# Which stages carry a decoder trunk's modulation rows, in which buffers, and the order at two stage ends

## The chip, the cores and the metric

The kernel runs on one core of one Trainium2 chip. The core has a matrix engine (PE, with a weight-load port of its own, PEld), a vector engine (DVE), a scalar engine (ACT), a general engine (POOL) and a sync engine (SP); each works through its own queue in order. Loads are issued from the SP and POOL queues and carried by 16 DMA engines. Tiles lie in on-chip memory, 128 partitions by so many elements; products accumulate in a second memory, PSUM (tiles named ps_...). The metric is the device time of one execution in microseconds (us); the median of several runs counts.

## The reference

Two layers, each a feed-forward block (half weight), a mixing block and another feed-forward block, on a sequence of 512 tokens with 1024 channels. Each block normalises its input and shifts and scales it; its output goes through a gate. These nine vectors of 1024 a layer, the modulation, come from one vector c:

```python
c_act = jax.nn.silu(c)
for l in range(DEPTH):                                   # 2
    mod = (c_act @ w_ada[l] + b_ada[l]).reshape(B, N_MOD, D_MODEL)      # 9 x 1024
    sh1, sc1, gt1, sh2, sc2, gt2, sh3, sc3, gt3 = [mod[:, i, None, :] for i in range(N_MOD)]
    hn = rms_norm(h, g_ffn1[l]) * (1.0 + sc1) + sh1
    h = h + 0.5 * (1.0 + gt1) * swiglu(hn, w_ffn1_in[l], w_ffn1_out[l])
    hn = rms_norm(h, g_mix[l]) * (1.0 + sc2) + sh2
    proj = hn @ w_mix_in[l]
    ...                            # attention, RWKV recurrence, short convolution, out product
    h = h + (1.0 + gt2) * mixed
    hn = rms_norm(h, g_ffn2[l]) * (1.0 + sc3) + sh3
    h = h + 0.5 * (1.0 + gt3) * swiglu(hn, w_ffn2_in[l], w_ffn2_out[l])
```

with `swiglu(x, w_in, w_out) = (silu(x @ w_in's first half) * (x @ w_in's second half)) @ w_out`, 2816 wide inside, all float32.

## The kernel before

**Tiling.** The state is kept transposed in eight tiles h of 128 x 512 (1024 channels by 512 tokens). Float32 products run as three products of a shorter format: every operand is split into a high part (wH, hnH, xs) and the rest (wL, hnL). `split` (L105 to L107) does this for a weight tile of 128 x 1024: ACT casts it to wH, DVE subtracts to get wL, PE uses wH, then wL.

**Stages.** In order: ffn1 of layer 0 (another routine, `ffn`), then for the rest mix 0, ffn2 of layer 0, ffn1 of layer 1, mix 1, ffn2 of layer 1. These three feed-forward stages are `ffn_whole`. It makes 22 column tiles of the wide product in pairs p = 0 to 10. Pairs 0 and 1 are done plainly (four column tiles j = 0 to 3, L1053 on; their stage start). Pairs 2 to 10 (`pair_in`) and the product back to 1024 channels (`out_product`) use Strassen-like sums: fewer products, with sums of weight blocks in their place, made by accumulating loads on POOL (`accum_op`) and by DVE additions. `out_product` runs seven products (A0, S, A1, S0, S1, S3, A3), each over six units u of two of the eleven row blocks k (the last unit has one); its weight row tiles are called rowk, 128 x 512.

**The modulation.** Each of its vectors is a column of eight values per partition; one value column needs one dot product on DVE (`ada_dot`, L170, a SCALAR_TENSOR_TENSOR of 128 x 1024 with an accumulated output): a 512 KB row tile of w_ada against silu(c) spread over the partitions (crow). 128 such rows remain for the kernel's stages after the start (`todo`), 16 having been done before. `ffn` of layer 0 does 48 of them beside its own work. `ffn_whole` does the rest by a plan (`ada_plan`, L197): DOTS says how many dots belong to each pair p, ROWS which of eight buffers b their row tiles use. The buffers are slots of later pairs' results (raw in the profile), so fewer are free toward the end. `load` issues a row's load on POOL for pairs up to one ahead, when its buffer has no earlier dot outstanding; `dots` puts each dot behind given instructions. In the table, DOTS[1] = (0, 6, 4, 4, 4, 4, 4, 4, 3, 2, 1): six dots at the plain start (two behind j = 2, four behind j = 3, L1074), then 30. DOTS[0], for the last stage, holds the last eight. Two crow tiles are loaded on SP, one for the six, one for the others. The mixes do no dots.

**Order.** A scheduler sets the order in most places from the code's order and its priorities, with buffers as constraints. At the end of the first two `ffn_whole` stages (`out_product`, L1016 on) the order is written by hand: `update` adds the block's result to h, `square` and `total` sum squares for the next norm, `stats` and `spread` make the reciprocal root (ACT's rstd, PE's ps_ss and ps_rstd), `apply` writes the next stage's normalised tiles hnH and hnL, `prepare` splits weights and sums of the remaining units, and `ahead` splits the first weight tiles of the stage that follows.

**The mix.** `products` (a generator in `mix`) yields the column tiles in the order of TILES: key, value, q0 to q3, lo, k0, r0, v0 and so on, weights from SP, while the attention and the two halves of the recurrence are interleaved. Tiles with tag u1 (four buffers) serve the second half of the recurrence later.

Of the kernel before, what the change touches and what calls it, by code (L numbers as in the profile page):

```python
# [36 lines left out]
DOTS = ((0, 0, 2, 2, 2, 2), (0, 6, 4, 4, 4, 4, 4, 4, 3, 2, 1))  # L37
ROWS = {1: (0, 1, 2, 3), 2: (0, 1, 2, 3), 3: (0, 1, 2, 3), 4: (2, 3, 4, 5), 5: (2, 3, 4, 5), 6: (4, 5, 6, 7), 7: (4, 5, 6, 7), 8: (5, 6, 7), 9: (6, 7), 10: (7,)}
# [24 lines left out]
def trunk_kernel(ctx, tc, ins, out, layers=L, phases=("ffn1", "mix", "ffn2")):  # L63
# [134 lines left out]
    def ada_plan(plan, bufs, crow):  # L198

        begun, last, marked = {}, [], set()  # L200
        turns = {}
        for p, n in enumerate(plan):
            for _ in range(n):
                own = ROWS[p]
                turns[p] = turns.get(p, -1) + 1
                last.append((p, own[(turns[p] + 2 * (p == 2 and plan[1] > 0)) % len(own)], todo.pop(0)))
        left, loaded, done = list(range(len(last))), {}, [0]
        rows = {}
# [10 lines left out]
        def dot(p, behind=None):  # L219
# [7 lines left out]
            with tc.issue_after(behind.ins) if behind else nullcontext():  # L227
                ada_dot(mod[l, i][:, k : k + 1], rows[n], crow[p > 1])
# [432 lines left out]
    def ffn_whole(l, w_in, w_pair, w_s, hn, im, ss, need, then, ready):  # L661
# [4 lines left out]
        with tc.tile_pool(name="act", bufs=1) as ap_:  # L666
# [66 lines left out]
            plan_ = DOTS[len(todo) > 8]  # L733
            crow = {}
            if plan_[1]:
                crow[False] = flat(R[1][:, 1])
                nc.sync.dma_start(crow[False], silu_c[0])
            load_rows, dot_ = ada_plan(plan_, [flat(R[n // 2][:, n % 2]) for n in range(4, 4 + 8)], crow)
# [74 lines left out]
            def out_product(rest):  # L813
# [19 lines left out]
                def load(name, u):  # L833
# [6 lines left out]
                    elif name == "S3":  # L840
                        for k in ks:
                            queued(nc.gpsimd, kept[k], block(one(k), 1, 0), accum_op=ALU.add)
# [155 lines left out]
                stats, spread, apply, low_, ahead = then()  # L998
                raws = [wp.tile([P, KD, P], F32, name="wraw", tag="wraw", bufs=2) for _ in range(2)]
                raws.append(flat(spare[3]).rearrange("p (k c) -> p k c", c=P))  # L1000

                def update(q, m):
                    pt = plan[q][2]
                    half, sl, _ = plan[q][4][0]
                    i = 4 * half + m
                    stt(h[i][:, sl], pt[m // 2][:, m % 2], cg[:, i : i + 1], h[i][:, sl], ALU.mult, ALU.add)
                    return square(i, sl)

                def total(sq, sl):
                    tt(ss[:, sl], ss[:, sl], sq, ALU.add)  # L1010
# [5 lines left out]
                with tc.manual_schedule(engines=HAND):  # L1016
# [6 lines left out]
                    sqs = [update(5, m) for m in range(4)]  # L1023
                    prepare(end)
                    for sq in sqs:
                        total(sq, hi_)
                    nothing(end)
                    stats(hi_)
# [22 lines left out]
                    return low_()  # L1051
# [3 lines left out]
            for p in range(NP):  # L1055
                if p < n_first:
                    X = R[p // 2][:, p % 2]
                    for i in range(2):
# [4 lines left out]
                        if not j:  # L1063
                            load_rows(0)
# [863 lines left out]
```

## Time and profile before

| | |
|---|---|
| median of three runs | 1916.5 us (1912.98 to 1918.74) |
| the profiled execution | 1911.23 us, span 1909.1 us, mean granted clock of PE 0.993 |
| ffn1 layer 0 | 0 to about 375 us |
| mix 0 | to about 620 |
| ffn2 layer 0 | to about 985; its pairs end near 857 |
| ffn1 layer 1 | to about 1340 |
| mix 1 | to about 1575 |
| ffn2 layer 1 | to the end |
| modulation rows loaded into raw | 80 x 512 KB, 6.7 us median from issue to landing |
| into wada (ffn1 layer 0) | 48 x 512 KB, 5.0 us |

How to read the rows: "PE L730 MATMUL ps_f<-comH,wL" is line 730's matmul, into ps_f, from comH and wL; in brackets how long the engine stood idle in front of it and what released it. "x66" counts instructions. In a window's row come its bounds, its length, busy time of PE, PEld, DVE, ACT and POOL with instruction counts, then PE's granted clock (1.00 is full speed), the busy share of the DMA engines and GB/s. A group's row has busy time, mean ns of one, then idle time before the group and its releaser.

### The profile page before, as it was taken

To read this page: it belongs to the slowest core of one execution; us is meant where nothing else is said; L and a number is where in the kernel's file an instruction comes from. 1 tells how busy PE (TensorE), PEld (TensorE's weight loads), DVE (VectorE), ACT (ScalarE), POOL (GpSimd) and SP (SyncE) were. 2 spreads that over 40 slices of the span, in tenths; PEclk is the share of its full clock that TensorE was granted. 3 is DMA by queue.
4 is the path that set the end of the run, shared out by engine and by line. 5 is a ranking of instruction groups with operands and counts; after the bars stand their busy time and mean duration, and the time that the engine had idled before them with its cause. 6 is when DMAs were issued, how large, how long until landed. Compare 5 with 4: busy or idle time off the path is not lost.

```text
span 1909.1 us, 39588 instructions
## 1 busy us (share of the span) xinstructions
PE 1845.2 (97%) x16468; PEld 1752.5 (92%) x16468; DVE 1530.9 (80%) x2432; ACT 918.3 (48%) x1412; POOL 191.9 (10%) x281
## 2 busy tenths in 40 slices
PE   9999999999999989999998999999999999999999
PEld 8998899987888989999988999999878889999999
DVE  7887677858876888989878897988588768777895
ACT  4453354355432545456644454655554334455564
POOL 0101101000000111110202121130000000110120
PEclk9999999999999999999999999999999999999999
DMA  7767867321221688875829786782221215775746
GB/s 311 251 175 246 254 196 242 138 70 64 64 80 41 241 239 249 243 200 169 200 111 289 230 243 173 219 212 65 82 62 54 88 53 155 200 184 159 225 111 156
DMA packets 112212, 322.01 MB, mean 169 GB/s; under 512 B 24096, under 2 KB 29216, under 8 KB 111008
## 3 DMA queue, kind: packets, MB, share of 16 engines
q1 hardware_dynamic: 73872, 190.75, 28.5%
q0 software_dynamic: 38160, 128.73, 27.7%
q8 instruction: 129, 2.11, 0.4%
q14 instruction: 51, 0.42, 0.1%
HBM read 315.50 MB, written 3.93 MB: 167 GB/s over the span
## 4 chain that ended last, share of the span: by engine, by line
PE 45%; DVE 21%; DMA 11%; issue 7%; ACT 3%; POOL 1%; SPq 0%; POOLq 0%; DVEq 0%; ACTq 0%
PE ps_mm L103 7%; DVE wL L107 6%; DMA raw<-in_wadaT 5%; PE ps_d L930 5%; PE ps_f L930 3%; PE ps_g L930 2%; PE ps_d L728 2%; PE ps_d L730 2%; PE ps_d L729 2%; PE ps_mm L96 2%; PE ps_mm L97 2%; PE ps_mm L95 2%; ACT wH L106 2%; PE ps_f L730 1%; PE ps_f L728 1%
## 5 line engine op out<-in xcount | busy, mean ns | idle before, releaser
L106 ACT CAST wH<-wraw 128x1024 fp32r<-128x1024 f32 (+2 forms) x210 | 207.2, 988 | 310.5 <-PE ps_mm L103 63.6
L107 DVE TENSOR_TENSOR wL<-wraw,wH 128x1024 fp32r<-128x1024 f32 (+2 forms) x210 | 238.9, 1140 | 54.5 <-ACT wH L106 54.1
L106 ACT CAST wH<-sum 128x1024 fp32r<-128x1024 f32 x153 | 160.7, 1050 | 160.4 <-DVE sum L790 74.4
L107 DVE TENSOR_TENSOR wL<-sum,wH 128x1024 fp32r<-128x1024 f32 x153 | 186.7, 1220 | 41.3 <-ACT wH L106 41.0
L103 PE MATMUL ps_mm<-hnH,wL 128*128 128x256 f32 x976 | 199.8, 283 | 3.6 <-DVE wL L107 3.6
L103 PE MATMUL ps_mm<-hnH,wH 128*128 128x256 f32 x976 | 197.7, 283 | 1.6 <-ACT silu L1066 1.2
L103 PE MATMUL ps_mm<-hnL,wH 128*128 128x256 f32 x976 | 197.6, 281 | 0.0
L728 PE MATMUL ps_d<-comH,wH 128*128 128x256 f32 x648 | 180.7, 279 | 3.2 <-DVE up L799 2.1
L730 PE MATMUL ps_d<-comH,wL 128*128 128x256 f32 x648 | 180.5, 279 | 3.3 <-DVE wL L107 3.3
L729 PE MATMUL ps_d<-comL,wH 128*128 128x256 f32 x648 | 180.0, 278 | 0.0
L103 PEld LDWEIGHTS ps_mm<-hnH,wL 128*128 128x128 f32 x976 | 149.7, 188 | 11.3 <-issue 6.6
L103 PEld LDWEIGHTS ps_mm<-hnH,wH 128*128 128x128 f32 x976 | 148.9, 188 | 9.5 <-issue 5.1
L103 PEld LDWEIGHTS ps_mm<-hnL,wH 128*128 128x128 f32 x976 | 149.7, 188 | 5.2 <-issue 4.9
L930 PE MATMUL ps_d<-xs,wH 128*128 128x256 f32 x792 | 137.2, 278 | 0.0
L728 PEld LDWEIGHTS ps_d<-comH,wH 128*128 128x128 f32 x648 | 122.8, 190 | 4.3 <-DVE up L799 2.7
L730 PEld LDWEIGHTS ps_d<-comH,wL 128*128 128x128 f32 x648 | 122.8, 189 | 4.0 <-DVE wL L107 3.7
L729 PEld LDWEIGHTS ps_d<-comL,wH 128*128 128x128 f32 x648 | 122.9, 190 | 0.0
L930 PEld LDWEIGHTS ps_d<-xs,wH 128*128 128x128 f32 x792 | 120.4, 190 | 0.1
L170 DVE SCALAR_TENSOR_TENSOR raw<-raw,crow 128x1024 f32<-128x1024 f32 x68 | 82.8, 1218 | 45.2 <-DMA raw<-in_wadaT 45.2
L930 PE MATMUL ps_d<-xs,wL 128*128 128x256 f32 x396 | 110.4, 279 | 3.8 <-DVE wL L107 3.8
L930 PE MATMUL ps_f<-xs,wH 128*128 128x256 f32 x528 | 90.3, 276 | 0.0
L217 POOL DMA_DIRECT2D raw<-in_wadaT x80 | 44.7, 572 | 427.0 <-DVE hn_t L293 192.6
(545 smaller groups left out, 5624.8 us busy)
## 6 DMA issues: line engine op xcount, KB each, us to landing
raw<-in_wadaT POOLq DMA_DIRECT2D x80, 512.0 KB, 6.7
wada<-in_wadaT POOLq DMA_DIRECT2D x48, 512.0 KB, 5.0
wraw<-in_wmi SPq DMA_DIRECT2D x38, 512.0 KB
wraw<-in_w2p SPq DMA_DIRECT2D x36, 512.0 KB
wraw<-in_w1p SPq DMA_DIRECT2D x32, 512.0 KB
sum<-in_w2s SPq DMA_DIRECT2D x20, 512.0 KB
sum<-in_w2s POOLq DMA_DIRECT2D x20, 512.0 KB, 9.0
wraw<-in_w1i SPq DMA_DIRECT2D x18, 512.0 KB
```

What stands on the lines that cost most here:

```text
L95: mm(acc, wH, xH, start=start, stop=False)
L96: mm(acc, wH, xL, start=False, stop=False)
L97: mm(acc, wL, xH, start=False, stop=stop)
L103: mm(acc[:, sl], w[a][:, k], x[b][:, sl], start=start and n == 0 and sl is HALVES[0], stop=stop and n == 2, skip_group_check=True)
L106: nc.scalar.copy(hi, src)
L107: return nc.vector.tensor_sub(lo, src, hi.bitcast(F32))
L170: stt(w, w, 1.0, crep, ALU.mult, ALU.mult, accum_out=out_)
L217: nc.gpsimd.dma_start(bufs[b], ins["wadaT"][l, i, k])
L728: mm(pt[:, i], wH, x[k][0], start=start and i + k == 0, stop=False, skip_group_check=True)
L729: mm(pt[:, i], wH, x[k][1], start=False, stop=False, skip_group_check=True)
L730: last = mm(pt[:, i], wL, x[k][0], start=False, stop=k == 3, skip_group_check=True)
L930: mm(pt[m // 2][:, m % 2], w[:, 4 * k + m], x[:, y, k], start=start and u + k + n + m % 2 == 0, stop=u == NU - 1 and n == 2, skip_group_ch ...
```

## The change

Four edits.

1. **Six dots move.** DOTS[1] becomes (0, 0, 4, ...): the plain start of ffn2 in layer 0 and of ffn1 in layer 1 has no dots, and the second crow tile is gone. Each mix does six, one behind each of its tiles q1, q2, q3, lo, k0 and r0 (MIX_DOTS), with four tiles of its own under tag u1: crow and three row tiles. Three rows and crow are loaded on POOL at the start, three more when a dot gives a buffer back. The total stays: 48 + 6 + 30 + 30 + 6 + 8 = 128.
2. **Row buffers.** ROWS is reordered: pair 3 uses (4, 5, 6, 7) while pair 2 uses (0, 1, 2, 3), and so on. The first loads are issued at j = 1, not j = 0.
3. **Three plain loads.** In product S3, row blocks k = 8, 9, 10 are loaded plainly on SP into a tile of their own, and DVE adds them to the kept ones; the other eight stay accumulating loads on POOL.
4. **Stage ends.** At the two hand-written ends, all four h updates of half a block come first, the weight work `prepare(end)` before the squares; `ahead(2)` moves up before `stats(hi_)`; `apply` has four tiles, not three, before the last unit. Before an ffn1 the table of silu is loaded right behind the last root. The stage doesn't return its leftover work as something that later weight fetches are held behind.

```diff
-DOTS = ((0, 0, 2, 2, 2, 2), (0, 6, 4, 4, 4, 4, 4, 4, 3, 2, 1))
-ROWS = {1: (0, 1, 2, 3), 2: (0, 1, 2, 3), 3: (0, 1, 2, 3), 4: (2, 3, 4, 5), 5: (2, 3, 4, 5), 6: (4, 5, 6, 7), 7: (4, 5, 6, 7), 8: (5, 6, 7), 9: (6, 7), 10: (7,)}
+DOTS = ((0, 0, 2, 2, 2, 2), (0, 0, 4, 4, 4, 4, 4, 4, 3, 2, 1))
+ROWS = {2: (0, 1, 2, 3), 3: (4, 5, 6, 7), 4: (2, 3, 4, 5), 5: (6, 7, 2, 3), 6: (5, 6, 7, 4), 7: (5, 6, 7, 4), 8: (5, 6, 7), 9: (6, 7), 10: (7,)}
+MIX_DOTS = ("q1", "q2", "q3", "lo", "k0", "r0")
...
                     elif name == "S3":
                         for k in ks:
-                            queued(nc.gpsimd, kept[k], block(one(k), 1, 0), accum_op=ALU.add)
+                            if k < NP - 3:
+                                queued(nc.gpsimd, kept[k], block(one(k), 1, 0), accum_op=ALU.add)
+                            else:
+                                y = row_tile(k)
+                                queued(nc.sync, y, block(one(k), 1, 0))
+                                tt(kept[k], kept[k], y, ALU.add)
...
-                    sqs = [update(5, m) for m in range(4)]
+                    update(5, range(4))
                     prepare(end)
-                    for sq in sqs:
-                        total(sq, hi_)
+                    sqs = squares(hi_, range(4))
+                    total(sqs, hi_)
                     nothing(end)
+                    ahead(2, raws[2])
                     stats(hi_)
...
-                    apply(hi_, range(3))
+                    apply(hi_, range(4))
                     for n, m in enumerate(unit(len(units) - 1)):
-                        sq = update(6, m)
-                        apply(hi_, range(3 + n, 4 + n))
-                        total(sq, lo_)
-                        if n == 1:
-                            ahead(2, raws[2])
+                        update(6, (m,))
+                        sqs = squares(lo_, (m,))
+                        if n < 3:
+                            apply(hi_, range(4 + n, 5 + n))
+                        total(sqs, lo_)
                     stats(lo_)
+                    if silu:
+                        act(E("none")[:, :1], vals["eps"], AF.Silu)
...
-                    return low_()
+                    low_()
+                    return ()
...
-                        if not j:
-                            load_rows(0)
+                        if j == 1:
+                            load_rows(1)
...
-                        for _ in range({2: 2, 3: 4}.get(j, 0)):
-                            dots(None, 1)
...
+            own = [U(1, n, [P, D]) for n in ("crow", "wada", "wada", "wada")]
+            load_rows, dot = ada_plan([(n, (n % 3,)) for n in range(len(MIX_DOTS))], own[1:], own)
+            load_rows(1)
+            nc.gpsimd.dma_start(own[0], silu_c[0])
...
+                if name in MIX_DOTS:
+                    dot(MIX_DOTS.index(name), got["moved"])
```

The first place is DVE's queue at the start of ffn2 in layer 0, where the plain column tiles end and pair 2 begins. The dots are the rows with mod_8 on the left (the number behind a name only tells instances apart); comL is an operand of the first pairs' products, sum and first are weight sums of pair 2. Before:

```order
L717 SCALAR_TENSOR_TENSOR q<-q,raw 128x512
L170 SCALAR_TENSOR_TENSOR raw,mod_8_7717<-raw 128x1024
L1067 SCALAR_TENSOR_TENSOR raw<-silu,ps_mm 128x512
L107 TENSOR_TENSOR comL<-q,comH 128x1024
L107 TENSOR_TENSOR wL<-wraw,wH 128x1024
L170 SCALAR_TENSOR_TENSOR raw,mod_8_7717<-raw 128x1024 x4
L107 TENSOR_TENSOR wL<-sum_7843,wH 128x1024
L107 TENSOR_TENSOR wL<-first,wH 128x1024
L762 TENSOR_TENSOR sum_7843<-sum_7843,first 128x1024
L107 TENSOR_TENSOR wL<-wraw,wH 128x1024
L1067 SCALAR_TENSOR_TENSOR raw<-silu,ps_mm 128x512
L170 SCALAR_TENSOR_TENSOR raw,mod_8_7717<-raw,crow 128x1024
```

and of the changed kernel:

```order
L712 SCALAR_TENSOR_TENSOR q<-q,raw 128x512
L108 TENSOR_TENSOR comL<-q,comH 128x1024
L712 SCALAR_TENSOR_TENSOR q<-q,raw 128x512
L108 TENSOR_TENSOR wL<-wraw,wH 128x1024
L1072 SCALAR_TENSOR_TENSOR raw<-silu,ps_mm 128x512
L108 TENSOR_TENSOR comL<-q,comH 128x1024
L108 TENSOR_TENSOR wL<-sum_7852,wH 128x1024
L108 TENSOR_TENSOR wL<-first,wH 128x1024
L753 TENSOR_TENSOR sum_7852<-sum_7852,first 128x1024
L171 SCALAR_TENSOR_TENSOR raw,mod_8_4397<-raw,crow 128x1024
L108 TENSOR_TENSOR wL<-wraw,wH 128x1024
L171 SCALAR_TENSOR_TENSOR raw,mod_8_4397<-raw,crow 128x1024
```

Before, five dots stand ahead of the split of the pair's first two sums, of which four in one row; now none does, and the first dot follows the addition behind them.

The second place is ACT's queue where ffn2 of layer 0 ends and ffn1 of layer 1 starts (sq are the squares, wHL and xs operands of the last units, hnH the next stage's normalised tiles, raw the third weight tile of that stage). Before, from the copies on and at the first silu:

```order
L963 COPY ps_g<-ps_d 128x512 x2
L257 ACTIVATE sq<-h_94 128x256
L257 ACTIVATE sq<-h_96 128x256
L257 ACTIVATE sq<-h_98 128x256
L257 ACTIVATE sq<-h_100 128x256
L106 CAST wHL<-sum 128x1024
L106 CAST xs<-raw 128x512
L275 ACTIVATE rstd<-ps_ss,v_eps 128x2
L106 CAST wHL<-sum 128x1024
L106 CAST xs<-raw 128x512
```

and of the changed kernel, at the same place:

```order
L959 COPY ps_g<-ps_d 128x512 x2
L107 CAST wHL<-sum 128x1024
L107 CAST xs<-raw 128x512
L252 ACTIVATE sq<-h_94 128x256
L252 ACTIVATE sq<-h_96 128x256
L252 ACTIVATE sq<-h_98 128x256
L252 ACTIVATE sq<-h_100 128x256
L107 CAST wH<-raw 128x1024
L270 ACTIVATE rstd<-ps_ss,v_eps 128x2
L107 CAST wHL<-sum 128x1024
L107 CAST xs<-raw 128x512
```

The cast of a weight sum and of xs stand ahead of the four squares now, and the next stage's weight tile is cast ahead of the root. Further on, the table load has moved, from (before)

```order
L275 ACTIVATE rstd<-ps_ss,v_eps 128x2
L294 ACTIVATE hnH<-hn_t,mod_0_8009 128x256 x9
L106 CAST wH<-wraws 128x1024
L106 CAST wH<-wraw 128x1024
L1066 ACT_TABLE_LOAD
L1066 ACTIVATE silu<-ps_mm 128x512 x2
```

to (after)

```order
L270 ACTIVATE rstd<-ps_ss,v_eps 128x2
L1049 ACT_TABLE_LOAD
L1049 ACTIVATE none<-v_eps 128x1
L289 ACTIVATE hnH<-hn_t,mod_0_8016 128x256 x9
L107 CAST wH<-wraws 128x1024
L107 CAST wH<-wraw 128x1024
L1071 ACTIVATE silu<-ps_mm 128x512 x2
```

The third place is DVE's queue at the start of mix 0, where the tiles key, value and q0 to q3 are made (rk and kt belong to the keys' norm, wada are the row tiles of the mix). Before:

```order
L107 TENSOR_TENSOR wL<-wraw,wH 128x1024
L1172 RECIPROCAL rk<-rk 128x512
L107 TENSOR_TENSOR wL<-wraw,wH 128x1024
L1173 SCALAR_TENSOR_TENSOR kt<-kt,gqk,rk 128x512
L107 TENSOR_TENSOR wL<-wraw,wH 128x1024 x4
L1201 RECIPROCAL rq<-rq 128x32
```

and of the changed kernel:

```order
L108 TENSOR_TENSOR wL<-wraw,wH 128x1024
L171 SCALAR_TENSOR_TENSOR wada_4169,mod_8_4397<-wada_4169,crow_4168 128x1024
L1179 RECIPROCAL rk<-rk 128x512
L171 SCALAR_TENSOR_TENSOR wada_4170,mod_8_4397<-wada_4170,crow_4168 128x1024
L1180 SCALAR_TENSOR_TENSOR kt<-kt,gqk,rk 128x512
L108 TENSOR_TENSOR wL<-wraw,wH 128x1024
L171 SCALAR_TENSOR_TENSOR wada_4171,mod_8_4397<-wada_4171,crow_4168 128x1024
L108 TENSOR_TENSOR wL<-wraw,wH 128x1024 x4
L1208 RECIPROCAL rq<-rq 128x32
```

Three of the six dots stand between the splits of the weights here, the first one ahead of the reciprocal; the other three come further on, behind lo, k0 and r0.

More of the change, by code (lines that the diff above doesn't have):

```diff
@@ L198, in ada_plan @@
     def ada_plan(plan, bufs, crow):
[L200 to L208, printed above, removed]
+        begun, last, done, rows = {}, [], [0], {}
+        for p, own in plan:
+            last.extend((p, b, todo.pop(0)) for b in own)
         def load(p):
@@ L227, in dot @@
             with tc.issue_after(behind.ins) if behind else nullcontext():
-                ada_dot(mod[l, i][:, k : k + 1], rows[n], crow[p > 1])
+                ada_dot(mod[l, i][:, k : k + 1], rows[n], crow[0])
                 if k == KD - 1 or n == len(last) - 1:
@@ L731, in prod @@
                 return last
[L733 to L738, printed above, removed]
+            crow = []
+            load_rows, dot_ = ada_plan([(p, ROWS[p][:n]) for p, n in enumerate(DOTS[len(todo) > 8]) if n], [flat(R[n // 2][:, n % 2]) for n in range(4, 4 + 8)], crow)
             def dots(behind, p):
@@ L998, in out_product, with update, squares, total @@
                 stats, spread, apply, low_, ahead = then()
+                silu = im == 6
                 raws = [wp.tile([P, KD, P], F32, name="wraw", tag="wraw", bufs=2) for _ in range(2)]
                 raws.append(flat(spare[3]).rearrange("p (k c) -> p k c", c=P))
-                def update(q, m):
+                def update(q, ms):
                     pt = plan[q][2]
                     half, sl, _ = plan[q][4][0]
[L1005 to L1010, printed above, removed]
+                    for m in ms:
+                        i = 4 * half + m
+                        stt(h[i][:, sl], pt[m // 2][:, m % 2], cg[:, i : i + 1], h[i][:, sl], ALU.mult, ALU.add)
+                def squares(sl, ms):
+                    return [square(4 + m, sl) for m in ms]
+                def total(sqs, sl):
+                    for sq in sqs:
+                        tt(ss[:, sl], ss[:, sl], sq, ALU.add)
                 def nothing(t):
@@ L1070, in ffn_whole @@
                         beside(2 * j + 1)
-                        for _ in range({2: 2, 3: 4}.get(j, 0)):
-                            dots(None, 1)
                 else:
                     if p == n_first:
-                        crow[True] = ap_.tile([P, D], F32, name="crow", tag="crep", bufs=1)
-                        nc.sync.dma_start(crow[True], silu_c[0])
+                        crow.append(ap_.tile([P, D], F32, name="crow", tag="crep", bufs=1))
+                        nc.sync.dma_start(crow[0], silu_c[0])
                     after[0] = loads[-2] if p <= n_first + 1 else None
@@ L1132, in shifted @@
             act(z, pt, AF.Copy, scale=got["om"][:, j : j + 1])
-            stt(z[:, 1:], pt[:, : T - 1], mu[:, j : j + 1], z[:, 1:], ALU.mult, ALU.add)
+            got["moved"] = stt(z[:, 1:], pt[:, : T - 1], mu[:, j : j + 1], z[:, 1:], ALU.mult, ALU.add)
             return z
@@ L1184, in products @@
                 elif kind == "q":
-                    nc.scalar.copy(qr[:, q], pt)
+                    got["moved"] = nc.scalar.copy(qr[:, q], pt)
                     sqs.append(E("qsq") if QE else S(q % 2, "qsq"))
```

## The prediction

> **What bounds the kernel now.** I read the page first, for the engine that is busy all the time, then the waits of that engine, then its timeline with the idle time in front of each row, and at every large wait the timeline of the engine that it waited for.
>
> ```profile
> span 1909.1 us, 39588 instructions
> PE 1845.2 (97%) x16468; PEld 1752.5 (92%) x16468; DVE 1530.9 (80%) x2432; ACT 918.3 (48%) x1412; POOL 191.9 (10%) x281
> PE ps_f L730 <- DVE wL L107: 10.0, 7, 4.4
> PE ps_f L728 <- ACT wH L106: 4.1, 2, 2.1
> ```
>
> The first two lines are the page's: PE is busy for 97% of the span. The other two are the waits of PE: the tile that waited, what it waited for, microseconds in total, times, longest. PE multiplies the same amount before and after, so only two things can be won: its idle time, 1909.1 - 1845.2 = 63.9 us, and time in which it runs at a lower granted clock. The largest wait is for the low half of a weight tile (wL, written by DVE). DVE is 80% busy over the span, so its queue is late in places, not everywhere. What is in front of wL in those places decides.
>
> **The start of ffn2 in layer 0, term by term.** PE's rows with the idle time in brackets, then DVE's:
>
> ```profile
> 653.13 0.50 PE L103 MATMUL ps_mm<-hnH,wL 128*128 128x256 f32 x2 [1.88 <-DVE wL L107]
> 671.43 0.38 PE L730 MATMUL ps_f<-comH,wL 128*128 128x256 f32 x1 [1.82 <-DVE wL L107]
> 679.20 0.39 PE L730 MATMUL ps_d<-comH,wL 128*128 128x256 f32 x1 [0.64 <-DVE wL L107]
> 704.47 0.38 PE L728 MATMUL ps_f<-hnH,wH 128*128 128x256 f32 x1 [2.04 <-ACT wH L106]
> 706.21 0.38 PE L730 MATMUL ps_f<-hnH,wL 128*128 128x256 f32 x1 [1.25 <-DVE wL L107]
> ```
> ```profile
> L170 DVE SCALAR_TENSOR_TENSOR raw<-raw,crow 128x1024 f32<-128x1024 f32 x68 | 82.8, 1218 | 45.2 <-DMA raw<-in_wadaT 45.2
> 669.00 1.22 DVE L170 SCALAR_TENSOR_TENSOR raw<-raw 128x1024 f32<-128x1024 f32 x1 [3.77 <-DMA raw<-in_wadaT]
> 700.91 1.23 DVE L170 SCALAR_TENSOR_TENSOR raw<-raw,crow 128x1024 f32<-128x1024 f32 x1 [5.04 <-DMA raw<-in_wadaT]
> ```
>
> The group shows 68 of the modulation dots: DVE stood 45.2 us in front of them, waiting for their 512 KB row tiles. The dot at 669.00 waited 3.77 us, four dots follow one another there, and the wL behind them was late for PE at 671.43. The dot at 700.91 waited 5.04 us, since its row goes into a buffer that an earlier dot of the same pair had just given back; an addition to a weight sum stood behind it, then ACT's cast of that sum (PE at 704.47), then wL (706.21). The change takes the six dots from this start and loads the rows of each of the pairs 2 to 8 into tiles that the pair before doesn't hold, so that all four of pair 3 can be loaded during pair 2. Removed: 1.82 + 0.64 + 2.04 + 1.25 = 5.75 us. The 1.88 us at 653.13 I leave in, because that weight tile came late itself and had only one dot in its neighbourhood.
>
> The clock adds to it. Windows of 8 or 9 us around the waits, PE's granted clock being the figure after the five busy times:
>
> ```profile
> 704.00:712.00 8.00, 6.28 (x38) 6.09 (x39) 7.97 (x9) 5.83 (x8) 1.75 (x2) 0.79 0.66 203
> 1024.00:1032.00 8.00, 7.89 (x54) 7.89 (x55) 7.97 (x12) 2.13 (x3) 2.60 (x4) 0.79 1.01 264
> 1057.00:1066.00 9.00, 6.87 (x33) 6.67 (x34) 8.59 (x12) 6.13 (x8) 1.39 (x2) 0.62 0.68 192
> 1298.00:1306.00 8.00, 6.38 (x40) 6.06 (x39) 7.49 (x11) 4.64 (x8) 0.00 (x0) 0.79 0.22 73
> 1626.00:1634.00 8.00, 5.43 (x33) 5.43 (x34) 5.96 (x6) 3.01 (x4) 0.00 (x0) 0.79 0.30 97
> ```
>
> At a mean of 0.79 over 8 us PE does 0.21 x 8 = 1.68 us less of work; at 0.62 over 9 us 3.42 us less. Each window holds one of the waits that the change removes, so I count 1.68 us with it: **term 1, 7.43 us**. What is late next here is that weight tile itself, or ACT's cast of it.
>
> The page "TensorE: Matmul & The Clock Gate" of the Trainium skill (section "What's actually happening") puts the fall of the clock behind an idle window of about 3.4 us, free-running. This trace doesn't bear out the length: four of the five windows are around waits of 1.62 to 2.70 us, and only the one at 1024 is around a longer one. If the rule held to the letter, those four falls of clock had another cause and would stay; that is a rival below.
>
> **The start of ffn1 in layer 1** has the same six dots and the same plan of rows, and a table load:
>
> ```profile
> 990.57 0.50 PE L103 MATMUL ps_mm<-hnH,wH 128*128 128x256 f32 x2 [1.18 <-ACT silu L1066]
> 1014.02 0.50 PE L103 MATMUL ps_mm<-hnH,wL 128*128 128x256 f32 x2 [1.09 <-DVE wL L107]
> 1024.11 0.39 PE L730 MATMUL ps_f<-comH,wL 128*128 128x256 f32 x1 [4.41 <-DVE wL L107]
> 1057.89 0.38 PE L728 MATMUL ps_f<-hnH,wH 128*128 128x256 f32 x1 [2.08 <-ACT wH L106]
> 1059.63 0.58 PE L730 MATMUL ps_f<-hnH,wL 128*128 128x256 f32 x1 [1.25 <-DVE wL L107]
> ```
> ```profile
> 988.62 1.28 ACT L1066 ACT_TABLE_LOAD   x1
> 1054.33 1.22 DVE L170 SCALAR_TENSOR_TENSOR raw<-raw,crow 128x1024 f32<-128x1024 f32 x1 [5.65 <-DMA raw<-in_wadaT]
> ```
>
> The waits are 1.18 + 1.09 + 4.41 + 2.08 + 1.25 = 10.01 us, the clock 1.68 + 3.42: **term 3, 15.11 us**. The table load of 1.28 us leaves the place where PE waited for the first silu. It now stands on ACT's queue at the end of the stage before, ahead of the last normalised tiles, which PE needs first; ACT is less than half busy, and I give back 0.6 us, between 0 and 1.28.
>
> **The two reordered stage ends.**
>
> ```profile
> 947.53 0.38 PE L930 MATMUL ps_d<-xs,wL 128*128 128x256 f32 x1 [1.64 <-DVE wL L107]
> 972.31 0.39 PE L97 MATMUL ps_mm<-hnH,wL 128*128 128x256 f32 x1 [0.76 <-DVE wL L107]
> 1300.75 0.39 PE L930 MATMUL ps_d<-xs,wL 128*128 128x256 f32 x1 [1.62 <-DVE wL L107]
> 1326.78 0.39 PE L97 MATMUL ps_mm<-hnH,wL 128*128 128x256 f32 x1 [0.76 <-DVE wL L107]
> ```
> ```profile
> 937.05 0.62 ACT L106 CAST wH<-rowk 128x512 fp32r<-128x512 f32 x1 [0.87 <-DMA rowk<-in_w2s]
> L863 DVE TENSOR_TENSOR sum<-sum,rowk 128x512 f32<-128x512 f32 x30 | 19.6, 683 | 0.0
> ```
>
> Up to 937 ACT's casts of row tiles wait for the adding loads, which run one behind another on POOL. Then the casts, their wL on DVE and the h updates come together, and PE waits at 947.53. With the last three rows loaded plain on SP, the casts come earlier; the price is three additions of 0.683 us on DVE in each of three stages. They stand before the crowded stretch, where DVE still waits for ACT, so nothing on the path; if that cover is gone 9 x 0.683 = 6.1 us. The wait at 972.31 is for the wL of the next stage's first tile, which now stands ahead of the normalisation. **Term 2: 1.64 + 0.76 = 2.40 us; term 4: 1.62 + 0.76 + 1.68 of clock = 4.06 us.**
>
> **ffn2 in layer 1** had no dots at its start, only the plan of rows changes:
>
> ```profile
> 1628.57 0.38 PE L730 MATMUL ps_d<-comH,wL 128*128 128x256 f32 x1 [2.70 <-DVE wL L107]
> 1668.17 0.39 PE L728 MATMUL ps_d<-comH,wH 128*128 128x256 f32 x1 [1.07 <-ACT ps_g L761]
> 1626.14 1.23 DVE L170 SCALAR_TENSOR_TENSOR raw<-raw,crow 128x1024 f32<-128x1024 f32 x1 [6.09 <-DMA raw<-in_wadaT]
> ```
>
> **Term 5: 2.70 + 1.07 + 1.68 = 5.45 us.** The rows that come earlier now share the DMA engines with the last weight tiles of the start; I give back 1.4 us, half of the 2.70, between 0 and 2.70.
>
> **What the mixes pay.** Six dots, seven loads of 512 KB on POOL and no more weights: 6 x (1.22 + 0.08) = 7.8 us of DVE in each mix, 15.6 in both.
>
> ```profile
> 395.00:410.00 15.00, 15.00 (x136) 14.87 (x133) 7.71 (x6) 6.28 (x10) 0.00 (x0) 1.00 0.44 153
> 445.00:470.00 25.00, 23.98 (x190) 18.61 (x189) 24.93 (x52) 13.80 (x33) 0.42 (x2) 1.00 0.07 23
> ```
> ```profile
> 1341.13 1.01 POOL L1523 MEMSET Sc<- 128x512 f32 x2 [53.81 <-DVE wL L107]
> 1345.51 3.35 DVE L1172 RECIPROCAL rk<-rk 128x512 f32<-128x512 f32 x1 [1.31 <-ACT rk L1171]
> 1348.78 1.16 DVE L107 TENSOR_TENSOR wL<-wraw,wH 128x1024 fp32r<-128x1024 f32 x1
> wada<-in_wadaT POOLq DMA_DIRECT2D x48, 512.0 KB, 5.0
> ```
>
> From 395 to 410 DVE is busy for 7.71 of 15 us and the DMA engines at 0.44, so the three dots that go there find room. From 445 to 470 it is busy for 24.93 of 25, and the last dot of the six meets that stretch: I charge its 1.30 us once in each mix, 2.6 us, between 0 and 15.6. The first dot waits for its row and for silu(c), whose loads start when the mix's buffers come free, at about 1341 in layer 1 (the memset's release). Row loads took 5.0 us, four together some 7 us by my estimate, so they are there at 1348; the reciprocal ends at 1348.86, the dot follows. The wL behind it slips by some 4 us at most. I charge nothing; the other end is a wait like the smallest of those above, 3.77 us in each mix, 7.5 us.
>
> **The sum.** 7.43 + 2.40 + 15.11 + 4.06 + 5.45 = 34.45 us less; 2.6 + 1.4 + 0.6 = 4.6 us back; -29.85 us. The profiled run, 1911.2 us with 2.1 around its span, would become 1881.4. The median shown is 1916.5, 5.3 above that run; from it **1886.7 us**.
>
> **Rivals.**
>
> A wait of the next kind takes the place (22%). 653.13 shows a weight tile that was late for PE by its own load. If the weight loads are next everywhere at the three starts, half of terms 1, 3 and 5 (27.99 us) stays: -29.85 + 14.0 = -15.9, **1900.6 us**. For it: the DMA engines are at 1.01 around 1024. Against it: at 700.91 and 1054.33 the engine that was late is DVE, standing before a row tile and nothing else.
>
> The falls of the clock stay (8%). PE's half-speed stretches are then not caused by the short waits: 10.14 us of clock less the 1.68 at 1024 is 8.46, -21.4, **1895.1 us**. Against it: each of them starts with a wait. This is what the Trainium skill's section named above would give.
>
> More than the sum (9%). The waits at pair 9 are of the same kind:
>
> ```profile
> 823.23 0.39 PE L730 MATMUL ps_g<-hnH,wL 128*128 128x256 f32 x1 [1.88 <-DVE wL L107]
> ```
>
> Their rows keep their lead, so I left them in. If earlier loads pull them forward too, in both stages with their clock, some 2 x (1.88 + 1.68) = 7 us go, and with the 4.6 us not paid it is -41.6, **1874.9 us**.
>
> The change moves nothing that counts (7%): DVE's time before the row tiles is slack, another wL comes as late, and the median stays within 0.3%, which is 5.75 us and about what a measurement of this kernel can tell from no change: **1916.5 us**.
>
> Slower (6%): DVE in the mixes. One dot behind a late row holds DVE for 1.30 + 3.77 = 5.07 us, and everything in a mix that is behind it: weight halves, then the recurrence, where DVE is full. The gain less the other charges is 32.45 us, so it decides from 32.45 / 5.07 = 6.4 of the twelve dots on. With all but the first of each mix, ten, it is 50.7 - 32.45 = +18.2, **1934.7 us**. Against it: the half-idle DMA engines and DVE in 395 to 410.
>
> **How the numbers follow.** The forecast has 48%, the rivals 22, 8, 9, 7 and 6. With all charges at their far ends (15.6, 7.5, 2.7, 1.28) the gain is 7.4, 1909; without any it is 1882, and the fourth case goes below that. The range is 1876 to 1908, which leaves out the unchanged and the slower case and the far tail of the two beside it. Faster by over 0.3%: 48 + 22 + 8 + 9 = 87%; same 7%; slower 6%.
>
> **What would show it.** Right: no PE wait over 1 us for wL or wH where 671.43, 704.47, 1024.11 and 1057.89 were, granted clock 1.0 in the windows of those places, DVE's time before dots down from 45.2 us to under 20, no table load before the first silu of ffn1 in layer 1, PE busy unchanged and its idle time down by some 20 us. Wrong: dots in the mixes with row waits of over 2 us, PE waits for wL between 400 and 475, or weight loads as the releaser at the stage starts. A mean granted clock that stays at 0.993 would speak for the second rival.

## The result, and the profile after

| | median | runs | profiled run: span, mean clock |
|---|---|---|---|
| before | 1915.64 us | 11 (1905.97 to 1923.98) | 1909.1 us, 0.993 |
| changed | 1904.77 us | 11 (1896.32 to 1912.62) | 1902.8 us, 0.990 |

The ratio is 0.9949 (95% interval 0.9926 to 0.9972): faster by half a per cent, 10.9 us, where 29.85 us and a time of 1886.7 us were forecast. The page's first lines and the waits of PE, after:

```profile
span 1902.8 us, 39607 instructions
PE 1845.1 (97%) x16468; PEld 1756.2 (92%) x16468; DVE 1535.1 (81%) x2443; ACT 916.0 (48%) x1413; POOL 185.2 (10%) x274
```
```profile
PE ps_f L926 <- DVE wL L108: 16.6, 4, 7.5
PE ps_d L725 <- DVE wL L108: 4.1, 2, 2.3
PE ps_q L1200 <- ACT qsq L1194: 3.4, 2, 2.3
...
PE ps_f L725 <- DVE wL L108: 2.4, 3, 1.4
```

PE is busy for as long as before, 1845.1 us, and its idle time fell from 63.9 to 57.7 us, where some 20 us were expected. The list of its waits is another: ps_f for wL at the pairs' products, 10.0 us before, is down to 2.4, and the waits for a cast wH there are gone. But a new one leads: ps_f at L926, a product of `out_product`, three long waits of 16.2 us together. And ps_q, in the mixes, is new.

To see where the time went, I cut the span at four rows of PE that exist in every kernel: the first ps_ks product of each mix, and the first product of each ffn2 (the one that waits for hnH, 1.03 us in most kernels and 1.62 us in e6, e9 and e11 below). "Middle" is ffn2 of layer 0 with ffn1 of layer 1; "last" is ffn2 of layer 1 to the span's end. All from one profiled execution each:

| us | to mix 0 | mix 0 | middle | mix 1 | last |
|---|---|---|---|---|---|
| before | 392.0 | 228.9 | 722.6 | 228.2 | 337.4 |
| changed | 395.6 | 229.3 | 704.8 | 231.4 | 341.7 |
| difference | +3.6 | +0.4 | -17.8 | +3.2 | +4.3 |

The first column has the same code in both. It lies between 391.6 and 396.8 in the fourteen profiles of this case, so some 5 us of a single run are chance, and the stages tell more than the spans. The middle gained, though less than the 29.0 us that terms 1 to 4 make. The last stage, from which 4 us were expected, lost 4.3.

The three long waits of PE have one form. They stand here with DVE, SP and POOL around the first (timeline rows: start, length, what, idle time in front and its releaser):

```profile
923.68 0.39 PE L926 MATMUL ps_f<-xs,wL 128*128 128x256 f32 x1 [4.50 <-DVE wL L108]
1266.96 0.58 PE L926 MATMUL ps_f<-xs,wL 128*128 128x256 f32 x1 [4.20 <-DVE wL L108]
1850.12 0.58 PE L926 MATMUL ps_f<-xs,wL 128*128 128x256 f32 x1 [7.54 <-DVE wL L108]
```
```profile
913.89 0.41 DVE L108 TENSOR_TENSOR xs<-raw,xs 128x256 fp32r<-128x256 f32 x1
921.80 0.69 DVE L838 TENSOR_TENSOR rowk<-rowk 128x512 f32<-128x512 f32 x1 [7.50 <-DMA rowk<-in_w2s]
922.41 1.22 DVE L108 TENSOR_TENSOR wL<-sum,wH 128x1024 fp32r<-128x1024 f32 x1
```
```profile
912.25 0.33 SPq L816 DMA_DIRECT2D sum<-in_w2s  x1
912.63 0.49 SPq L816 DMA_DIRECT2D rowk<-in_w2s  x1
```
```profile
910.18 7.09 POOL L816 DMA_DIRECT2D rowk<-in_w2s  x8 [0.45 <-DVE wL L108]
```

DVE stands for 7.50 us in front of the addition at L838, the third of the new ones (k = 10). Its row is issued on SP only at 912.63, behind a weight sum, and lands nearly 9 us later, with the weight sum and eight accumulating loads from POOL under way beside it. The wL that PE needs stands right behind the addition. In the last stage it is the other two rows, k = 8 and 9:

```profile
1846.28 0.69 DVE L838 TENSOR_TENSOR rowk<-rowk 128x512 f32<-128x512 f32 x1 [8.94 <-DMA rowk<-in_w2s]
1848.24 0.69 DVE L838 TENSOR_TENSOR rowk<-rowk 128x512 f32<-128x512 f32 x1 [1.27 <-DMA rowk<-in_w2s]
```
```profile
1829.77 4.10 SPq L816 DMA_DIRECT2D out<-h  x4
1833.92 2.25 SPq L816 DMA_DIRECT2D rowk<-in_w2s  x2
```

There SP first issues four stores of the output, each of which waits for an update of h, and the row loads are behind them. Three windows around the three waits (PE's granted clock is the figure after the five busy times):

```profile
920.00:930.00 10.00, 6.32 (x41) 6.32 (x42) 8.20 (x13) 1.68 (x4) 0.00 (x0) 0.83 1.10 260
1264.00:1274.00 10.00, 7.04 (x40) 7.04 (x41) 8.92 (x14) 1.66 (x3) 0.00 (x0) 0.66 1.10 260
1846.00:1862.00 16.00, 11.88 (x81) 11.88 (x82) 13.03 (x19) 3.77 (x7) 1.72 (x2) 0.69 0.87 176
```

The clock takes 1.7 + 3.4 + 5.0 us beside the waits' 4.50 + 4.20 + 7.54: 26 us at most. Some 3 us of it are counted twice: read us by us, the clock is at 0.50 already for the last 1.6 us before 1266.96 and the last 4.5 us before 1850.12, while PE still stands. The DMA engines are full in the first two windows (a share of 1.10). The page "DMA: Bandwidth & Descriptors" of the Trainium skill (section "Issuing engines are not separate DMA queues") says that loads run on the same 16 engines whichever engine issues them; this trace agrees, since SP's plain row had no quicker way: it took nearly 9 us to land, and the rows from POOL between 905 and 926 us took 7.9 to 16.6 us.

The theory from here on: edit 3 costs what the other edits gain beyond 10.9 us, because an addition on DVE waits in the queue for its load, which an accumulating load doesn't. The rivals: the place is short of loads whichever queue carries them; or the other edits are worth less than was forecast.

### The profile page after: what moved, and what is told of

It reads as the page before. It is cut to its first block, busy times and chain, and to the rows that moved or that the text cites. A ratio compares the mean times of both kernels' runs of the same rounds, so it can differ in the third digit from the quotient of the medians.

```text
span 1902.8 us, 39607 instructions
## 1 busy us (share of the span) xinstructions
PE 1845.1 (97%) x16468; PEld 1756.2 (92%) x16468; DVE 1535.1 (81%) x2443; ACT 916.0 (48%) x1413; POOL 185.2 (10%) x274
## 4 chain that ended last, share of the span: by engine, by line
PE 60%; DVE 20%; DMA 10%; issue 6%; ACT 3%; POOL 1%; SPq 0%; DVEq 0%; POOLq 0%; ACTq 0%
PE ps_mm L104 13%; PE ps_d L926 5%; DVE wL L108 5%; PE ps_mm L97 3%; PE ps_mm L96 3%; PE ps_mm L98 3%; PE ps_g L926 3%; PE ps_f L926 3%; PE ps_d L723 3%; PE ps_d L725 3%; PE ps_d L724 3%; DMA raw<-in_wadaT 2%; DMA rowk<-in_w2s 2%; PE ps_f L725 1%; PE ps_f L723 1%
## 5 line engine op out<-in xcount | busy, mean ns | idle before, releaser
L926 PE MATMUL ps_d<-xs,wH 128*128 128x256 f32 x792 | 136.5, 277 | 0.0
L926 PEld LDWEIGHTS ps_d<-xs,wH 128*128 128x128 f32 x792 | 119.9, 188 | 0.0
L171 DVE SCALAR_TENSOR_TENSOR raw<-raw,crow 128x1024 f32<-128x1024 f32 x68 | 82.5, 1217 | 34.8 <-DMA raw<-in_wadaT 33.5
L926 PE MATMUL ps_d<-xs,wL 128*128 128x256 f32 x396 | 109.9, 277 | 0.0
L926 PE MATMUL ps_f<-xs,wH 128*128 128x256 f32 x528 | 98.0, 290 | 0.0
L926 PE MATMUL ps_f<-xs,wL 128*128 128x256 f32 x264 | 77.2, 292 | 16.6 <-DVE wL L108 16.6
```

The lines of the kernel that those rows point to most:

```text
L171: stt(w, w, 1.0, crep, ALU.mult, ALU.mult, accum_out=out_)
L926: mm(pt[m // 2][:, m % 2], w[:, 4 * k + m], x[:, y, k], start=start and u + k + n + m % 2 == 0, stop=u == NU - 1 and n == 2, skip_group_ch ...
```

## The experiments

Ratios go by runs of before on the same chip, whose median was 1912.63 us for e9, e10 and e11, 1916.27 for e12 and 1915.2 to 1915.5 for the others; the stages are cut as above, from one profiled execution each. e10 leaves the mixes' dots out, so it is there for their price alone.

| kernel | median | ratio to before (95%) | mix 0 | middle | mix 1 | last |
|---|---|---|---|---|---|---|
| S3 accumulating (e1) | 1887.66 | 0.9851 (0.9815 to 0.9887) | 231.4 | 696.2 | 237.2 | 331.5 |
| before + edit 3 (e2) | 1933.54 | 1.0095 (1.0064 to 1.0125) | 228.7 | 731.2 | 230.5 | 349.0 |
| k = 8, 9 plain (e3) | 1903.72 | 0.9930 (0.9904 to 0.9955) | 229.6 | 698.7 | 235.8 | 340.2 |
| k = 10 plain (e12) | 1897.31 | 0.9894 (0.9852 to 0.9936) | 231.5 | 705.7 | 234.2 | 332.5 |
| k = 8, 9 plain, not in last (e5) | 1890.26 | 0.9879 (0.9859 to 0.9900) | 229.8 | 699.2 | 230.8 | 333.3 |
| before + row buffers (e4) | 1899.45 | 0.9921 (0.9894 to 0.9949) | 230.8 | 716.7 | 228.2 | 333.8 |
| before + moved dots (e8) | 1910.66 | 0.9975 (0.9957 to 0.9993) | 232.3 | 709.7 | 235.7 | 338.0 |
| e1, ends of before (e7) | 1896.14 | 0.9895 (0.9866 to 0.9924) | 229.6 | 703.7 | 230.3 | 333.2 |
| e1, mix dots later (e6) | 1886.87 | 0.9858 (0.9839 to 0.9876) | 232.7 | 694.0 | 231.5 | 333.4 |
| e1, mix dots between (e11) | 1889.01 | 0.9875 (0.9857 to 0.9893) | 231.0 | 700.4 | 240.1 | 332.0 |
| e1, no mix dots (e10) | 1881.82 | 0.9837 (0.9813 to 0.9861) | 228.4 | 692.4 | 228.0 | 332.9 |
| e5 + e11 (e9) | 1893.48 | 0.9895 (0.9868 to 0.9923) | 232.9 | 706.4 | 233.5 | 331.8 |

Where the code of a stage is the same, its times still differ from profile to profile: 692.4 to 700.4 us in the middle (e1, e6, e10, e11), 331.5 to 333.4 in the last stage (e1, e5, e6, e7, e9, e10, e11), 229.3 to 232.3 in mix 0 and 230.3 to 237.2 in mix 1 (the changed kernel, e1, e3, e5, e7, e8 and e12). A difference of two single stages is good to no better than that.

**Edit 3 taken out, and alone.**

```diff
-                            if k < NP - 3:
-                                queued(nc.gpsimd, kept[k], block(one(k), 1, 0), accum_op=ALU.add)
-                            else:
-                                y = row_tile(k)
-                                queued(nc.sync, y, block(one(k), 1, 0))
-                                tt(kept[k], kept[k], y, ALU.add)
+                            queued(nc.gpsimd, kept[k], block(one(k), 1, 0), accum_op=ALU.add)
```

> The changed kernel with S3's last three row blocks back to accumulating loads on POOL; all else as changed. Theory (the plain row of k = 10 lands some 9 us after its issue and its addition holds DVE's queue): the waits of PE for ps_f's wL in out_product (4.50, 4.20 and 7.54 us in the changed kernel) and the clock lost with them (1.7 + 3.4 + 5.0 us) go, some 5 us of the waits of before come back at the stage ends: about 21 us less than the changed kernel, span near 1882. Rival (the loads as a whole are the limit there, whichever queue issues them): the same product waits for the same rows, span within 6 us of 1903.

> The kernel before with the three plain loads of S3 alone. Theory: the three waits appear here too, some 26 us with their clock, less some 5 us of waits that it removes: about 20 us slower than before, span near 1929. Rival (the waits need the changed stage ends or the changed rows): within 5 us of before, on either side.

Without edit 3 the median is 1887.66 us, 17.1 us under the changed kernel's; the middle is 8.6 us shorter and the last stage 10.2. Edit 3 alone makes the kernel before slower: 18.4 us in the medians (1933.54 against 1915.16), again 8.6 in the middle and 11.6 in the last stage. So its price is about the same with the other edits and without them, and the rival that the place is short of loads anyway falls. The waits of e2, and of e1, where no wait at L921 (its `out_product`) is long:

```profile
PE ps_f L935 <- DVE wL L107: 15.9, 3, 8.0
PE ps_f L730 <- DVE wL L107: 13.3, 9, 4.6
PE ps_f L728 <- ACT wH L106: 4.7, 3, 2.6
```
```profile
PE ps_q L1195 <- ACT qsq L1189: 6.4, 2, 3.2
PE ps_d L725 <- DVE wL L108: 4.4, 2, 2.6
...
PE ps_g L921 <- DVE wL L108: 2.4, 6, 0.8
```

A late row as such is not what costs. In e1 the adding load of k = 10, the last of POOL's, is issued only at 925.80, when the plain row of the changed kernel had long landed (921.80), and ACT's casts wait for such rows, as here for 1.85 us:

```profile
925.80 0.86 POOL L816 DMA_DIRECT2D rowk<-in_w2s  x1 [1.79 <-DMA rowk<-in_w2s]
928.09 0.62 ACT L107 CAST wH<-rowk 128x512 fp32r<-128x512 f32 x1 [1.85 <-DMA rowk<-in_w2s]
```

Yet PE's longest wait from there to 1000 us is 0.62 us. What costs is that the addition stands on DVE's queue ahead of a wL that is due sooner. An addition further back on that queue, or a plain load issued earlier, was not tried.

**Which of the three rows.**

```diff
-                            if k < NP - 3:
+                            if k not in (NP - 3, NP - 2):                  (e3)
+                            if k != NP - 1:                                (e12)
+                            if ss is None or k not in (NP - 3, NP - 2):    (e5: ss is None in the last stage)
```

> The changed kernel with k = 8 and 9 plain and k = 10 accumulating on POOL as before. Theory (only the load of k = 10 is late, since it stands on SP's queue behind a weight sum that waits for its buffer): as fast as the kernel with all three accumulating, or up to 3 us faster, span 1879 to 1883. Rival (the additions on DVE or plain loads as such cost): between the two, span 1888 to 1897, with a wait of DVE in front of an addition.

> The changed kernel with only k = 10 plain in S3, k = 8 and 9 accumulating. Theory (in the two stages that are followed by another, the one load of k = 10 is late, since it stands behind a weight sum on SP's queue and lands among the accumulating loads; in the last stage it is not that one but k = 8 and 9): PE's waits of about 4.5 and 4.2 us at ps_f with their clock (1.7 and 3.4 us) appear in the first two, none over 1 us in the last: 10 to 14 us more than with all accumulating, median 1897 to 1902. Rival (the wait comes from three additions and three loads together): 1888 to 1892.

> The changed kernel with k = 8 and 9 plain in the two stages that another feed-forward or mix stage follows, all else of S3 accumulating; in the last stage nothing plain. Theory (in the last stage the two plain loads stand on SP's queue behind stores of the output, which wait for the h updates, and DVE's addition waits 9.2 us; in the others they land early): PE's wait of 7.83 us in the last stage and some 5 us of clock go against the kernel with two plain loads everywhere, span 1882 to 1886, median 1884 to 1889. Rival (plain loads cost at other places, too): median 1892 or more.

My first answer, that only k = 10 is late, held for the two middle stages and missed the last: e3 has 698.7 us in the middle, but 340.2 in the last stage, where DVE stood 9.21 us in front of k = 8:

```profile
1841.41 0.69 DVE L838 TENSOR_TENSOR rowk<-rowk 128x512 f32<-128x512 f32 x1 [9.21 <-DMA rowk<-in_w2s]
1843.45 0.69 DVE L838 TENSOR_TENSOR rowk<-rowk 128x512 f32<-128x512 f32 x1 [1.34 <-DMA rowk<-in_w2s]
```

e12 is the other half: k = 10 alone brings waits of 2.48 and 3.26 us in the middle (705.7 us), less than the 4.5 and 4.2 expected, and none over 0.6 us for a weight in the last stage (332.5). The halves don't add up in the medians: e3 is 16.1 us above e1 and e12 9.7, together more than the 17.1 of all three rows, and e3's profiled run is 5.3 us below its median. Where each row costs is read from the waits; how the price divides among them stays open. In e5 both late cases are gone, 1890.26. It isn't better than e1: of edit 3 nothing is left that gains, and the waits at the stage ends that I put down to the accumulating loads don't need them changed, since e1 has none over 0.9 us there.

**The other edits, one by one.**

```diff
-ROWS = {1: (0, 1, 2, 3), 2: (0, 1, 2, 3), 3: (0, 1, 2, 3), 4: (2, 3, 4, 5), ...
+ROWS = {1: (0, 1, 2, 3), 2: (0, 1, 2, 3), 3: (4, 5, 6, 7), 4: (2, 3, 4, 5), 5: (6, 7, 2, 3), ...     (e4, on before)
```

> The kernel before with the reordered row buffers alone (the six dots stay at the starts with buffers 0 to 3). Theory (row waits in front of dots late in a pair make PE's waits at 704, 1058 and 1628 of before): these go, some 15 us with their clock, and some 5 us of new row waits at pair 5 come, as in the changed kernel at 751 and 1093: 8 to 12 us less than before. Rival (the gain of the first two long stages is that of the moved dots and of the stage ends): within 3 us of before.

> The kernel before with the six dots in the mixes alone (the first rows of the pairs are loaded at j = 1; row buffers, S3 and stage ends as before). Theory: the waits at the two starts go (some 10 us with clock), those of late rows at 704, 1058 and 1628 stay, each mix pays about 2 us: 6 to 10 us less than before, and some 10 us more than with the new row buffers. Rival (the mixes pay what the starts gain): within 4 us of before.

> The kernel with S3 all accumulating and with the stage ends of before, so moved dots and row buffers only. Theory (the reordered ends take away the waits of before at 947, 972, 991, 1301 and 1327): 5 to 8 us more than with the new ends, 1893 to 1896. Rival (those waits were made by what comes before the ends): within 2 us of it.

In the middle, moving the dots takes 722.6 to 709.7 (12.9 us), the row buffers on top to 703.7 (6.0; alone on before 5.9), the new ends to 696.2 (7.5). The steps make 26.4 us by the way they are taken, and each has the spread given above. By the medians the same steps are worth 4.8 us (the dots), 14.5 (the row buffers; alone 15.7) and 8.5 (the ends), so the row buffers look like the largest gain, though the intervals, some 5 us either way, don't set them clear of the ends. (e4 leaves the first loads at j = 0; they move with the dots, in e8.) In the last stage the row buffers give 4.8 us on top of the dots and 3.6 alone, the dots nothing. e8 is worth 4.8 us only as a whole, below the 6 to 10 expected: its mixes are 3.4 and 7.5 us longer than before, though in part by chance, since other profiles of the same mixes are up to 3.0 and 5.4 us shorter. e4's median gain of 15.7 us is above the 8 to 12 expected; its stages show 9.5 without mix 0, but the profiled run is the slowest of its seven (1892 to 1907). In e7 the waits of before at the ends are back, four nearly whole (0.76, 1.17, 1.38 and 0.75 us) and the first smaller (0.61 where 1.64 was). The first silu's:

```profile
987.35 0.50 PE L104 MATMUL ps_mm<-hnH,wH 128*128 128x256 f32 x2 [1.17 <-ACT silu L1057]
```

**The dots in the mixes.**

```diff
-MIX_DOTS = ("q1", "q2", "q3", "lo", "k0", "r0")
+MIX_DOTS = ("q3", "lo", "k0", "r0", "v0", "c0")     (e6)
+MIX_DOTS = ("q2", "q3", "lo", "k0", "r0", "v0")     (e11, e9)
...
-            load_rows, dot = ada_plan([(n, (n % 3,)) for n in range(len(MIX_DOTS))], own[1:], own)
+            def dot(n, behind):                         (e10)
+                l_, i, k = todo.pop(0)
+                ts(mod[l_, i][:, k : k + 1], prm(l_, "b_ada")[:, at : at + 1], 1.0, None, ALU.mult)
```

> The kernel with S3 all accumulating, leaving out the twelve dots of the mixes, their loads and silu(c): those columns of the modulation hold the bias alone. It prices the dots in their new place. Theory (the dots delay the weight splits and the attention: mixes of 231.4 and 237.2 us in the profile with them, against 228.9 and 228.2 before): 4 to 8 us less than with them, 1880 to 1884, mixes of 228 to 230. Rival (DVE had room for them, and the longer mixes are chance): within 2 us of 1887.7.

> The kernel with S3 all accumulating, with the six dots of each mix behind q3, lo, k0, r0, v0 and c0. Theory (three dots between the weight splits give the two weight buffers back late, the next weight tile is loaded late, and PE waits 3.2 us in each mix for the squares of q3): those waits go, 4 to 6 us less than with the dots as changed, 1882 to 1884. Rival (DVE is full from 445 to 470 and the dots only move their cost there): 3 to 8 us more than with the dots as changed.

> The kernel with S3 all accumulating, with the mix dots behind q2, q3, lo, k0, r0 and v0. Theory (there is no free place for the sixth: three early cost a late weight tile, two late ones cost the end of the recurrence): waits of 1 to 2 us at both places, within 3 us of the two other placements, 1884 to 1890. Rival (only the third early dot and the last late one cost): both waits gone, 1880 to 1883.

> The same dots, with k = 8 and 9 plain in the two stages that are followed by another. A version that might beat both kernels: some 1884 to 1889, well below the changed kernel's 1904.8; the two plain rows are worth nothing that can be measured, by the theory that only a row that DVE waits for costs. Rival: the spread of the runs with plain loads (to 1899 at e5) shows again, median 1890 or more.

Without the dots both mixes are back at 228 us. Their price isn't sharp. The medians of e1 and e10 are 5.8 us apart (1887.66 and 1881.82), but e10 ran on a chip where before was faster, too: against their own runs of before they gain 27.5 and 30.8 us, so 3.3. e11, on e10's chip, is 7.2 us above e10. Both mixes together take 464.1 us in the mean of the seven profiles with the dots as changed (459.9 to 468.6) and 457.9 in that of the four without any (456.4 to 459.2), 6.2 us. So it is 3 to 7 us, and where the dots stand made no difference that these runs can tell. In the changed kernel three early dots delay the weight splits, and the weight buffers come back late. DVE, then ACT, of mix 0:

```profile
401.99 1.16 DVE L171 SCALAR_TENSOR_TENSOR wada<-wada,crow 128x1024 f32<-128x1024 f32 x1
...
403.74 1.22 DVE L108 TENSOR_TENSOR wL<-wraw,wH 128x1024 fp32r<-128x1024 f32 x1
404.88 1.22 DVE L171 SCALAR_TENSOR_TENSOR wada<-wada,crow 128x1024 f32<-128x1024 f32 x1
...
406.02 1.22 DVE L108 TENSOR_TENSOR wL<-wraw,wH 128x1024 fp32r<-128x1024 f32 x1
```
```profile
409.10 1.05 ACT L107 CAST wH<-wraw 128x1024 fp32r<-128x1024 f32 x1 [5.29 <-DMA wraw<-in_wmi]
...
413.44 1.04 ACT L107 CAST wH<-wraw 128x1024 fp32r<-128x1024 f32 x1 [2.31 <-DMA wraw<-in_wmi]
```

The split that before ended 6.5 us after the mix's first ps_ks ends 9.4 us after it. There are two buffers for raw weights, so the load of a next tile, free to start only then, is late for ACT, the tile q3 is late for PE, and its squares for ps_q. With the dots later (e6) that wait is gone and another stands at the end of the recurrence:

```profile
PE ps_mm L104 <- DVE y L1513: 6.5, 2, 3.3
PE ps_f L725 <- DVE wL L108: 3.4, 4, 1.4
```

Two of e6's dots in mix 0, at 447 and 467 us, stand in the full stretch of DVE which the prediction named; that PE's wait at 606 follows from them is my reading and isn't shown. e6 and e1 can't be told apart (1886.87 and 1887.66); e11 has both waits in mix 1 (3.09 and 3.17 us, where 1 to 2 were expected) and gains nothing; e9, meant to be the best at 1884 to 1889, is no better than e1 with its 1893.48. **e1 and e6 beat both kernels**: the changed kernel with all of S3's loads left accumulating, 0.9851 and 0.9858 of before.

## Why the prediction was wrong

**The step that failed** is in the two reordered stage ends: "They stand before the crowded stretch, where DVE still waits for ACT, so nothing on the path; if that cover is gone 9 x 0.683 = 6.1 us." The three additions were priced by how long they run, 0.683 us, and not by what they wait for. Each can be a new wait on DVE's queue, for a row tile: four of the nine stood for 7.50, 7.20, 8.94 and 1.27 us in the changed kernel, with the wL that PE needed next behind them. The runs showed 17.1 us (e1) and 18.4 us (e2) for them, three times the far end that I gave. That far end isn't in my sum of the far ends either: with it the slow end is 1915 us, not 1909. What I had to do was to ask of each of the nine rows what stands ahead of it on SP and when it lands: a weight sum and eight accumulating loads in the middle stages, four stores of the output in the last. The prediction even says that up to 937 "ACT's casts of row tiles wait for the adding loads". It took the queue on POOL for the cause; in e1 these casts wait as before, and PE doesn't wait for them.

Without that edit the forecast would have held: e1 is at 1887.66 us, 27.5 us under its own runs of before, against 1886.7 and 29.85. So close a number is partly luck, as its terms missed both ways. By its steps:

- Terms 1 to 4 (29.0 us in the middle): 26.4 in e1, 22.2 to 30.2 in the four profiles with this middle. The ends gave 7.5, where 2.40 + 4.06 and the table load's 1.18 make 7.6. Dots and row buffers gave 18.9 of 21.4. The waits named at 671, 704, 1024 and 1058 are gone. Two smaller ones came that I hadn't foreseen (2.61 and 1.76 us in e1), behind late rows at pair 5, which takes buffers 2 and 3 from pair 4; in the changed kernel:

```profile
748.44 1.22 DVE L171 SCALAR_TENSOR_TENSOR raw<-raw,crow 128x1024 f32<-128x1024 f32 x1 [4.51 <-DMA raw<-in_wadaT]
```

- So the row waits went only in part: DVE still stands 34.8 us in front of 68 dots, not under 20 as I had put it (45.2 before):

```profile
L171 DVE SCALAR_TENSOR_TENSOR raw<-raw,crow 128x1024 f32<-128x1024 f32 x68 | 82.5, 1217 | 34.8 <-DMA raw<-in_wadaT 33.5 <-DMA crow<-silu_c 1.3
```

That most of those left lie at places where PE has operands in hand I take from the list of PE's waits; it isn't shown dot by dot.

- Term 5 (5.45 less 1.4 us in the last stage): 5.9 in e1, 4.0 to 5.9 in the seven profiles with this last stage, 3.6 to 4.8 for the row buffers alone. Right within the spread; whether a share of it went back to the weight loads can't be told.
- The mixes (2.6 us): 3 to 7 us. Their bounds held. The last dot runs at 445.27, where the full stretch begins, but no run prices it alone. What the sum left out is the weight buffer: I wrote that the wL behind the dots "slips by some 4 us at most" and charged nothing, without asking which load that slip holds back.
- The table load (0.6 us): it runs behind the last root, and in e1 no wait of PE over 0.9 us follows there, so little of it comes back.
- The clock: in e1 it stays at 1.00 at the places of the five falls, so that rival falls, but what a wait costs in clock is partly chance (below).
- The rivals: the measured 1904.8 us lies nearest to the first one's 1900.6, but not by its mechanism, as the releaser at the stage starts isn't a weight load. The slower side had its place in the mixes; it was S3 where an addition behind a late row held DVE, the very pattern of that rival.

## What to carry to other kernels

An addition that replaces an accumulating load puts a wait on an engine that serves others in order: price it by when its load lands, in every stage in which the code runs, and by what stands behind it, not by its length. And where work delays a step that frees a buffer, follow the buffer to the next load, because with two of them a slip of a few microseconds comes back as a late transfer.

## What the runs showed of the hardware

The granted clock answers to waits of like length in unlike ways. In e1 PE waited 3.22 us for qsq in mix 0 and the clock stayed full; it waited 3.19 us at the same product in mix 1 and the clock was low over the next two windows:

```profile
415.00:425.00 10.00, 9.82 (x75) 8.20 (x76) 4.27 (x16) 2.75 (x6) 0.00 (x0) 1.00 0.15 53
1334.00:1351.00 17.00, 13.81 (x73) 9.97 (x72) 4.88 (x6) 5.99 (x9) 0.00 (x0) 0.73 0.45 160
1351.00:1376.00 25.00, 24.91 (x187) 22.30 (x186) 16.65 (x43) 14.66 (x38) 0.00 (x0) 0.91 0.13 43
```

That is 17 x 0.27 + 25 x 0.09 = 6.8 us, and explains most of e1's long mix 1. In the changed kernel the same product waited 2.27 us and the clock stayed full:

```profile
1344.00:1361.00 17.00, 14.73 (x114) 11.92 (x113) 7.54 (x18) 6.61 (x10) 0.00 (x0) 1.00 0.39 142
1361.00:1386.00 25.00, 24.03 (x188) 20.91 (x189) 19.12 (x45) 18.39 (x52) 0.00 (x0) 1.00 0.20 65
```

Before, a wait of 1.62 us at 1301 had a fall behind it. The Trainium skill's page "TensorE: Matmul & The Clock Gate" (section "What's actually happening") has the clock follow a free-running window, and the traces show such a grid. In windows of 0.25 us one sees the clock fall to 0.50 and come back; the figure of the window that it changes in gives the moment, here 1301.15 and 1304.57:

```profile
1301.00:1301.25 0.25, 0.25 (x4) 0.25 (x4) 0.25 (x1) 0.25 (x1) 0.00 (x0) 0.81 0.00 0
1304.50:1304.75 0.25, 0.25 (x4) 0.25 (x4) 0.25 (x2) 0.00 (x0) 0.00 (x0) 0.87 0.05 16
```

Read so, the falls of before come at 707.24, 1024.67, 1058.81, 1178.28, 1301.15 and 1628.84 us, which are 93, 10, 35, 36 and 96 steps of 3.413 us apart. Each lasts one step, the one at 1058.81 two, e1's in mix 1 four. In all fourteen profiles every fall and return behind the first 16 us lies on one such grid for the run, to 0.02 us. So the place of a wait on the grid counts: e1's wait in mix 1 has 2.15 us inside one step, the one in mix 0 no more than 1.7 us in either of two. That isn't the whole rule, since before a wait of 1.88 us at 823.23 lies inside one step, too, and had no fall; what else counts stays open. A step at half clock costs 1.7 us, and from 30 us on the profiles hold from none (e5, e7) to 44 us at half clock (e2). A sum of such terms is thus uncertain by some microseconds a run, and the spread of the runs of one kernel (16 us over the eleven of the changed one) agrees with that.
